# A softmax on negated scores with the attention sink as a 129th column of each head's tile

## The chip, the cores and the metric

The kernel runs on one core of a Trainium2 chip. The metric is the device time of one execution in microseconds (us). The kernel before takes 1183.58 us, the median of three runs (1183.52 to 1184.87).

A core has five engines with a queue of instructions each, which start in order and wait for each other through semaphores: TensorE (PE in the profile; the loading of its weights has a row of its own, PEld), VectorE (DVE), ScalarE (ACT), GpSimd (POOL) and SyncE (SP, which here issues DMAs).

## What is computed

One decoder layer on 1024 positions of width 1024 in float32: two token mixers on one input projection, and behind them a convolutional gated MLP. The change lies in the first mixer, sliding-window attention with 8 query heads, 2 key heads, head width 64 and a window of 128 positions in blocks of 128. Each head has a learned sink: one more score, which takes part in the softmax and has no value row.

```python
scores = jnp.einsum('bnqhgd,bnkhd->bnhgqk', qb, kb) * (HEAD_DIM ** -0.5)
alibi = -slopes[:, :, None, None] * dist[None, None]
scores = jnp.where(valid, scores + alibi, NEG_INF)
probs = jax.nn.softmax(jnp.concatenate([scores, sink], axis=-1), axis=-1)[..., :-1]
out = jnp.einsum('bnhgqk,bnkhd->bnqhgd', probs, vb)
```

## The kernel before, in words

The program runs in stages: the key, value and query projections (to some 50 us), the attention (some 50 to 180 us, with the projection of u and then of the second mixer's v woven in), and the second mixer, gates, merge and MLP to the end. Matrix products are made from a high and a low part of each operand (three products in place of one), so each product is preceded by a split: ScalarE writes the high part (copy_hi, L89), VectorE or GpSimd subtracts it from the value for the low part.

The attention is a loop over sixteen softmax blocks: two halves of four heads, and in each half eight blocks of 128 queries. Since a query sees 128 keys, of the block before and its own, the scores of both key blocks are merged into one tile of 128 columns per head. The tile c holds 128 queries (partitions) by four heads by 128 columns, with three buffers.

The loop (L647 to 685) is written out by hand as a software pipeline, and each engine runs its part in that order. Pass n holds, in this order:

- s_mm(n): scores on TensorE into PSUM (tile sc, two matmul lines, L439 and L442).
- s_mask(n): VectorE merges the two halves (L457) and adds the distance penalty ali, which gives c (L458). In blocks 0 and 8, which have no block before them, it is one addition (L453) and a selection on GpSimd (L454).
- s_exp(n-1): four exponentials on ScalarE, one for each head, with the negated maximum as bias and an accumulated sum (L476); the exponential of the sink's part (L478); on VectorE the sum of both (L479) and the reciprocal (L480); on GpSimd the multiplication of c by it (L481).
- s_max(n): VectorE's maximum over 128 columns (L465), the minimum of its negative and of the negated sink (L466), and sink minus maximum (L467). These last two and L479 work on 128 partitions by 4 numbers, with both inputs in SBUF.
- pv_mm(n-4): probabilities times values on TensorE (L517).
- filler: pieces of other projections on TensorE, by the table FILL.
- p_trans(n-2): four transposes of c on TensorE (L487), in which c is the operand that is loaded as weights and ident the moving one.
- pv_out(n-4): ScalarE copies half of the product (tile o, L527), VectorE adds the other half into ya (L530).
- the norm of new q: a square on ScalarE (L276), a sum and a scaling on VectorE (L281, L282), a power on GpSimd (L283).
- p_split(n-2): the split of the transposed probabilities (ch on ScalarE by L89, cl on VectorE, L496), and on GpSimd four selections that part them into the two key blocks (eh, ch, el, cl; L503 and L505).
- weights(n): the split of loaded weights, with the subtraction on GpSimd (L110, L193). A buffer that it frees is loaded again by SyncE (L99).
- the projection u times rstd_b on VectorE (uT, L679) in passes where it is complete; q's transposes and split for block n+2 (L295, L89, L304), and the q norm's product (qr, L289).

So on VectorE, L479 and L480 of block n-1 stand between L458 and L465 of block n. On ScalarE, the exponentials of block n-1 stand behind the split of q for block n+1. On GpSimd, L481 stands ahead of the power, the selections and the subtractions of its pass. PSUM tiles of TensorE's next product come free when VectorE or ScalarE has read them.

Of the kernel before, what the change touches and what calls it, by code (L numbers as in the profile page):

```python
# [10 lines left out]
F = mybir.dt.float32  # L11
R = mybir.dt.float32r
U8 = mybir.dt.uint8
AF = mybir.ActivationFunctionType
ALU = mybir.AluOpType
AX = mybir.AxisListType
# [7 lines left out]
NEG = -1e30  # L24
# [10 lines left out]
def build(tc, a):  # L35
    nc = tc.nc
    ctx = ExitStack()
    with ctx, tc.manual_schedule(engines={mybir.EngineType.PE}):
        body(ctx, tc, nc, a)


def body(ctx, tc, nc, a):
    L, H = slice(0, 512), slice(512, 1024)
    base = ctx.enter_context(tc.tile_pool(name="base", bufs=1))
# [6 lines left out]
    def nm(s):  # L51
        uid[0] += 1
        return f"{s}_{uid[0]}"
# [26 lines left out]
    def PH(s):  # L80
        if psum.get("H") is None:
            return PS(s)[:, 0:512]
        return psum["H"].tile([128, 512], F, tag="H", name=nm(s))
# [30 lines left out]
    cp = base.tile([128, 194], F, name="cp")  # L114
    sink_b = base.tile([128, 8], F, name="sink_b")
# [19 lines left out]
    def rms_rows(pb, col, hs=(0, 1)):  # L135
# [6 lines left out]
        for h, p in zip(hs, pb):  # L142
# [12 lines left out]
    kgq = at.tile([128, 1], F, name="kgq")  # L155
    eps_x = at.tile([128, 8], F, name="eps_x")
    nsink = at.tile([128, 8], F, name="nsink")
# [8 lines left out]
    ali = kp.tile([128, 8, 128], F, name="ali")  # L166
    nc.gpsimd.affine_select(out=ali[:, 0:4, :], in_=rstd_b[:, 0:128].unsqueeze(1).to_broadcast([128, 4, 128]),
                            pattern=[[0, 4], [1, 128]], compare_op=ALU.is_gt, fill=0.0, base=0,
                            channel_multiplier=-1)
# [57 lines left out]
    for k in range(8):  # L227
# [3 lines left out]
        for c in xcuts[k] if k in xcuts else (slice(0, 512), slice(512, 1024)):  # L231
# [3 lines left out]
                                           op0=ALU.mult, op1=ALU.subtract)  # L235
        for s in range(8):
            o = pkv[s // 4][:, (s % 4) * 256:(s % 4 + 1) * 256]
            c = slice(s * 128, (s + 1) * 128)
# [22 lines left out]
    st = {}  # L261
# [62 lines left out]
    q_proj(1)  # L324
    ss8 = pa.tile([128, 8], F, name="ss8")
    nc.vector.tensor_scalar(nsink, sink_b, -1.0, None, op0=ALU.mult)
    nc.vector.tensor_scalar(kgq, cp[:, 184:185], cp[:, 185:186], 0.125, op0=ALU.mult, op1=ALU.mult)
    nc.vector.tensor_copy(ss8, p_ssq[:, 0:16].rearrange("p (s two) -> p s two", two=2)[:, :, 0])
    rsqrt_cols(rstd, ss8, 8, D)
    nc.vector.tensor_scalar(eps_x, ss8, EPS / D, EPS * EPS, op0=ALU.mult, op1=ALU.add)  # L330
# [1 line left out]
    for h in range(2):  # L332
# [3 lines left out]
                                axis=AX.X, op=ALU.add)  # L336
# [87 lines left out]
    tm = tm_cm.__enter__()  # L424
# [21 lines left out]
    def s_mask(n):  # L446

        half, b = divmod(n, 8)
        p4 = st.pop(("ps", n))
        hs = slice(4 * half, 4 * half + 4)  # L450
        c = tm.tile([128, 4, 128], F, tag="c", name=nm("c"), bufs=3)
        if b == 0:
            nc.vector.tensor_tensor(c, p4[:, :, 0:128], ali[:, hs, :], op=ALU.add)  # L453
            nc.gpsimd.affine_select(out=c, in_=c, pattern=[[0, 4], [-1, 128]], compare_op=ALU.is_ge,  # L454
                                    fill=NEG, base=0, channel_multiplier=1)
        else:
            nc.vector.copy_predicated(p4[:, :, 128:256], msk, p4[:, :, 0:128])  # L457
            nc.vector.tensor_tensor(c, p4[:, :, 128:256], ali[:, hs, :], op=ALU.add)  # L458
        st[("c0", n)] = c

    def s_max(n):
        hs = slice(4 * (n // 8), 4 * (n // 8) + 4)
        c = st.pop(("c0", n))
        sm = tm.tile([128, 4, 4], F, tag="sm", name=nm("sm"), bufs=3)
        nc.vector.tensor_reduce(sm[:, 0, :], c, axis=AX.X, op=ALU.max)  # L465
        nc.vector.scalar_tensor_tensor(sm[:, 0, :], sm[:, 0, :], -1.0, nsink[:, hs], op0=ALU.mult, op1=ALU.min)  # L466
        nc.vector.tensor_tensor(sm[:, 2, :], sink_b[:, hs], sm[:, 0, :], op=ALU.add)  # L467
        st[("c", n)] = (c, sm)

    last_exp, last_sel = [None], [None]  # L470

    def s_exp(n):
        c, sm = st[("c", n)]
        m, den, es = sm[:, 0, :], sm[:, 1, :], sm[:, 2, :]
        for i in range(4):
            last_exp[0] = nc.scalar.activation(c[:, i, :], c[:, i, :], AF.Exp, bias=m[:, i:i + 1],  # L476
                                               accum_out=den[:, i:i + 1])
        nc.scalar.activation(es, es, AF.Exp)  # L478
        nc.vector.tensor_tensor(den, den, es, op=ALU.add)  # L479
        nc.vector.reciprocal(den, den)  # L480
        nc.gpsimd.tensor_tensor(c, c, den.unsqueeze(2).to_broadcast([128, 4, 128]), op=ALU.mult)  # L481

    def p_trans(n):
        c = st.pop(("c", n))[0]
        p = PH("pt")
        for i in range(4):
            nc.tensor.transpose(p[:, i * 128:(i + 1) * 128], c[:, i, :], ident)  # L487
        st[("pt", n)] = p.rearrange("p (h q) -> p h q", q=128)
# [158 lines left out]
    for n in range(20):  # L647
        if n < 16:
            s_mm(n)
            s_mask(n)  # L650
        if 0 <= n - 1 < 16:
            s_exp(n - 1)
        if n < 16:
            s_max(n)
# [3 lines left out]
        if 0 <= n - 2 < 16:  # L658
            p_trans(n - 2)
# [1318 lines left out]
def layout(x, mix_norm, w_in, q_norm, k_norm, sinks, sgu_norm, w_s, b_s,  # L1978
           w_oa, w_ob, w_out, ffn_norm, w_up, conv_w, conv_b, w_down):
    c = np.ascontiguousarray  # L1980
    x, w_in, w_oa, w_ob, w_out = (np.asarray(t)[0] for t in (x, w_in, w_oa, w_ob, w_out))
    w_up, w_down, conv_w, conv_b = (np.asarray(t)[0] for t in (w_up, w_down, conv_w, conv_b))
    mix_norm, ffn_norm, q_norm, k_norm = (np.asarray(t)[0] for t in (mix_norm, ffn_norm, q_norm, k_norm))
    sinks, sgu_norm, w_s, b_s = (np.asarray(t)[0] for t in (sinks, sgu_norm, w_s, b_s))

    def tiles(w, nk):
        n = w.shape[1] // 128
        return c(w.reshape(nk, 128, n, 128).transpose(2, 1, 0, 3))

    def pairs(w):  # L1990
        t = w.reshape(2, 2, 128, 4, 2, 128).transpose(4, 0, 2, 3, 1, 5).reshape(2, 2, 128, 1024)
        return np.stack([t[0, 1], t[0, 0], t[1, 0], t[1, 1]])

    def rows(w):
        return c(w.reshape(2, 4, 128, 2, 256).transpose(3, 2, 0, 1, 4).reshape(2, 128, 2, 8, 128))

    qcols = np.concatenate([np.arange(h * 64, h * 64 + 64) for h in HP])
    xT = x.T.reshape(8, 128, S)
    wk = w_in[:, 512:768].reshape(8, 128, 256)
    up_order = np.stack([np.arange(NPAIR), np.arange(NPAIR) + NPAIR], 1).reshape(-1)  # L2000
    wup = tiles(w_up, 8)[up_order]

    def pcol(v):
        return v.reshape(-1, 128).T

    cwp = conv_w.reshape(3, 44, 128)[:, up_order].transpose(2, 1, 0).reshape(128, 132)
    cbp = pcol(conv_b)[:, up_order]
    bsr = np.repeat(b_s.reshape(4, 2, 128).transpose(1, 0, 2).reshape(2, 512), 64, axis=0)
    qk = np.stack([np.tile(q_norm, 2), np.tile(k_norm, 2)], axis=1)
    q = np.arange(128)[:, None]  # L2010
    j = np.arange(128)[None, :]
    dist = np.where(j <= q, q - j, q - j + 128).astype(np.float32)
    slopes = np.array([2.0 ** -(h + 1) for h in SP], np.float32)
    ali = -slopes[None, :, None] * dist[:, None, :]
    return {
        "xw": c(np.concatenate([mix_norm.reshape(8, 128, 1), wk, xT], axis=2)),
        "wq": rows(w_in[:, qcols]),
        "wvs": rows(w_in[:, 1280:1792]),
        "wu": tiles(w_in[:, 768:1280], 8),
        "wga": tiles(w_in[:, 1792:2816], 8),  # L2020
        "wgb": tiles(w_in[:, 2816:3840], 8),
        "wb": c(np.stack([pairs(w_ob), pairs(w_oa[qcols])])),
        "wout": tiles(w_out, 8),
        "wup": wup,
        "wdown": c(w_down.reshape(NPAIR, 128, 1024)),
        "ws": c(w_s.transpose(2, 0, 1)),
        "cp": c(np.concatenate([pcol(ffn_norm), cwp, cbp, qk, pcol(mix_norm)], axis=1)),
        "sink": c(np.broadcast_to(sinks[SP], (128, 8))),
        "rb": c(np.concatenate([np.broadcast_to(sgu_norm, (128, 512)), bsr], axis=1)),
        "ident": np.eye(128, dtype=np.float32),  # L2030
        "ali": c(ali),
    }
# [13 lines left out]
```

## Time and profile before

| | |
|---|---|
| median of 3 runs | 1183.58 us (1183.52 to 1184.87) |
| span of the profiled execution | 1183.5 us |
| TensorE busy | 1170.3 us (99%) |
| weight load | 990.4 us (84%) |
| VectorE | 874.5 us (74%) |
| ScalarE | 566.5 us (48%) |
| GpSimd | 631.8 us (53%) |

The profiled execution's own time is its span, 1183.5 us; the median of the runs lies 0.1 us beside it. Times in rows of a timeline are us from the span's start; a row has start, length, engine, line, operation, output and inputs by tile name, shapes, and in brackets how long the engine stood idle before and what ended that. A group row has a count, then busy time and mean ns. PE's busy time is that of overlapping matmuls, so a busy PE is not PE at its peak.

### The profile page before, as it was taken

The page shows a single profiled execution, that of the slowest core. Times are in us where ns is not written, and L with a number is a line of the kernel's source. Part 1 is how long each engine was busy: PE and PEld are TensorE (multiplying, and loading weights), DVE is VectorE, ACT ScalarE, POOL GpSimd, SP SyncE. Part 2 cuts the span into 40 slices and gives each one's busy share as a digit, 9 for nine tenths or more (in the row PEclk, how much of TensorE's full clock was granted, in tenths as well). Part 3 has the DMA queues.
Part 4 walks back from the last instruction along what each step waited for, and adds up shares of the span by engine and source line. Part 5 has one row for each costly group of instructions (what it writes and reads, how often), then busy time and mean ns, then how long its engine had stood idle before and what let it go on. Part 6 is the DMA issues. An engine that isn't in the chain of part 4 may idle for free.

```text
span 1183.5 us, 15928 instructions
## 1 busy us (share of the span) xinstructions
PE 1170.3 (99%) x5842; PEld 990.4 (84%) x5842; DVE 874.5 (74%) x1037; ACT 566.5 (48%) x878; POOL 631.8 (53%) x435
## 2 busy tenths in 40 slices
PE   8999999999999999999999999999999999999998
PEld 8989989988888878888878888888888888888887
DVE  7798975743536776678788788877888797875674
ACT  8555667644336653335444443444444445425331
POOL 2467685488884764444867677776767541000000
PEclk9999999999999999999999999999999999999999
DMA  7110136157556654454545445455555268975471
GB/s 272 37 55 19 54 130 228 56 168 239 161 160 204 233 193 154 146 176 132 138 129 169 118 149 152 142 141 134 166 137 160 72 219 287 365 232 196 155 231 67
DMA packets 80942, 188.66 MB, mean 159 GB/s; under 512 B 9184, under 2 KB 16864, under 8 KB 80736
## 3 DMA queue, kind: packets, MB, share of 16 engines
q1 hardware_dynamic: 73008, 167.58, 40.7%
q0 software_dynamic: 7456, 15.73, 8.0%
q10 hardware_dynamic: 400, 4.33, 1.1%
q8 instruction: 46, 0.75, 0.3%
q14 instruction: 32, 0.26, 0.1%
HBM read 146.97 MB, written 49.02 MB: 166 GB/s over the span
## 4 chain that ended last, share of the span: by engine, by line
PE 82%; DVE 4%; POOL 3%; ACT 2%; issue 2%; DMA 1%; DVEq 0%; POOLq 0%; SPq 0%; ACTq 0%
PE pz L1060 50%; PE pd L1855 10%; PE pdy L1855 8%; PE px L95 2%; PE px L93 2%; PE px L94 2%; PE pu L95 1%; PE pu L93 1%; PE pu L94 1%; PE pv L517 1%; PE pq L93 1%; PE pq L95 1%; PE pq L94 1%; DVE xa L621 1%; DMA lq<-wup 0%
## 5 line engine op out<-in xcount | busy, mean ns | idle before, releaser
L1060 PE MATMUL pz<-T,qh 128*128 128x512 f32 x472 | 145.6, 390 | 0.0
L1060 PE MATMUL pz<-B,ph 128*128 128x512 f32 x352 | 109.7, 393 | 0.7 <-ACT x L1695 0.7
L1060 PEld LDWEIGHTS pz<-T,qh 128*128 128x128 f32 x472 | 88.4, 188 | 18.6 <-ACT u L885 0.3
L1019 POOL TENSOR_TENSOR pl<-lp,ph 128x1024 fp32r<-128x1024 f32 x30 | 73.2, 2439 | 52.9 <-ACT ph L89 52.9
L1060 PE MATMUL pz<-T,ql 128*128 128x512 f32 x236 | 91.8, 389 | 0.0
L1019 POOL TENSOR_TENSOR ql<-lq,qh 128x1024 fp32r<-128x1024 f32 x30 | 76.8, 2559 | 9.1 <-ACT qh L89 9.1
L1060 PEld LDWEIGHTS pz<-B,ph 128*128 128x128 f32 x352 | 65.1, 188 | 16.7 <-ACT x L1695 3.8
L1078 DVE TENSOR_TENSOR pz<-pz,rstd_b 128x1024 f32<-128x1024 f32 x60 | 73.9, 1232 | 4.6 <-ACT rstd_b L143 2.5
L1060 PE MATMUL pz<-T,s3h 128*128 128x512 f32 x232 | 71.4, 389 | 0.0
L1060 PE MATMUL pz<-y,wjh 128*128 128x512 f32 x224 | 69.5, 391 | 0.6 <-POOL y L1233 0.3
L1060 PE MATMUL pz<-B,pl 128*128 128x512 f32 x176 | 68.6, 390 | 0.0
L1855 PE MATMUL pd<-bh,ah 128*128 128x512 f32 x176 | 68.5, 389 | 0.0
L1855 PE MATMUL pd<-bl,ah 128*128 128x512 f32 x176 | 68.5, 389 | 0.0
L1855 PE MATMUL pd<-bh,al 128*128 128x512 f32 x176 | 68.5, 389 | 0.0
L1060 PE MATMUL pz<-T,AX 128*128 128x512 f32 x264 | 63.4, 389 | 0.0
L1060 PE MATMUL pz<-B,AX 128*128 128x512 f32 x264 | 63.4, 389 | 0.0
L1019 POOL TENSOR_TENSOR s3l<-lq,s3h 128x512 fp32r<-128x512 f32 x20 | 26.0, 1298 | 62.3 <-ACT s3h L89 62.3
L1060 PEld LDWEIGHTS pz<-T,AX 128*128 128x128 f32 x264 | 49.5, 188 | 10.3
L1060 PEld LDWEIGHTS pz<-B,AX 128*128 128x128 f32 x264 | 49.6, 188 | 10.3
L89 ACT ACTIVATE AX<-lr 128x1024 fp32r<-128x1024 f32 x22 | 23.4, 1063 | 70.9 <-POOL lr L621 70.9
L621 DVE TENSOR_TENSOR pz<-pz,u 128x512 f32<-128x512 f32 x37 | 25.9, 700 | 42.5 <-ACT u L1072 36.2
L1550 DVE SCALAR_TENSOR_TENSOR tg<-pz,cp,tg 128x1023 f32<-128x1023 f32 (+1 forms) x44 | 56.2, 1278 | 0.8
(359 smaller groups left out, 3597.6 us busy)
## 6 DMA issues: line engine op xcount, KB each, us to landing
lp<-wup SPq DMA_DIRECT2D x22, 512.0 KB, 3.8
lq<-wup SPq DMA_DIRECT2D x22, 512.0 KB, 4.2
ra<-wdown SPq DMA_DIRECT2D x44, 256.0 KB, 4.9
b<-T SPq DMA_DIRECT2D x44, 256.0 KB, 3.5
lq<-wup POOLq DMA_DIRECT2D x42, 256.0 KB, 5.3
B<-tv SPq DMA_DIRECT2D x33, 256.0 KB, 2.0
T<-tt SPq DMA_DIRECT2D x33, 256.0 KB, 2.1
b<-B SPq DMA_DIRECT2D x33, 256.0 KB, 3.0
```

Source lines behind the costliest of these rows:

```text
L89: return nc.scalar.activation(dst, src, AF.Copy, scale=scale)
L93: nc.tensor.matmul(out, wh, mh, start=first, stop=False, **kw)
L94: nc.tensor.matmul(out, wh, ml, start=False, stop=False, **kw)
L95: nc.tensor.matmul(out, wl, mh, start=False, stop=last, **kw)
L517: nc.tensor.matmul(o, vhl[:, kb, g, :], w[:, 2 * g:2 * g + 2, :], start=i == 0 and g == 0, stop=i == len(ops) - 1, skip_group_check=True)
L621: eng.tensor_tensor(out, x, y, op=op)
L1019: nc.gpsimd.tensor_tensor(l, r, h.bitcast(F), op=ALU.subtract)
L1060: nc.tensor.matmul(o, p[:, k, :], m, start=not more and k == 0 and j == 0, stop=k == nk - 1 and j == 2, skip_group_check=True)
L1078: nc.vector.tensor_tensor(z, z, rstd_b, op=ALU.mult)
L1550: nc.vector.scalar_tensor_tensor(t[:, j:], p[:, 0:1024 - j], cw[:, ci, 2 - j:3 - j], t[:, j:], op0=ALU.mult, op1=ALU.add)
L1855: nc.tensor.matmul(o[d], p[:, k - k0, m], q[:, k - k0, :], start=new and k == 0 and j == 0, stop=k == HK - 1 and j == 2, skip_group_check= ...
```

## The change

The scores are negated from the start: the factor 0.125 in kgq, which scales the keys, becomes -0.125, the host's table ali changes sign, and the masked value in blocks 0 and 8 becomes positive. The tile c gets a 129th column for each head (its rows now start every 516 bytes instead of 512; the tile has 2064 bytes on each partition instead of 2048), into which ScalarE copies the negated sink at the start of s_mask. One minimum over 129 columns replaces the maximum and the two operations behind it. The exponentials run over 129 columns with scale -1, so that their accumulated sum holds the sink's part; the sink's own exponential and the addition go. The operations on the 128 score columns (L454, L458, L481, the transposes) now work on rows with a gap of one column.

```diff
-    nc.vector.tensor_scalar(kgq, cp[:, 184:185], cp[:, 185:186], 0.125, op0=ALU.mult, op1=ALU.mult)
+    nc.vector.tensor_scalar(kgq, cp[:, 184:185], cp[:, 185:186], -0.125, op0=ALU.mult, op1=ALU.mult)
...
-        c = tm.tile([128, 4, 128], F, tag="c", name=nm("c"), bufs=3)
+        cs = tm.tile([128, 4, 129], F, tag="c", name=nm("c"), bufs=3)
+        c = cs[:, :, 0:128]
+        nc.scalar.copy(cs[:, :, 128], nsink[:, hs])
...
-                                    fill=NEG, base=0, channel_multiplier=1)
+                                    fill=-NEG, base=0, channel_multiplier=1)
...
     def s_max(n):
-        hs = slice(4 * (n // 8), 4 * (n // 8) + 4)
-        c = st.pop(("c0", n))
-        sm = tm.tile([128, 4, 4], F, tag="sm", name=nm("sm"), bufs=3)
-        nc.vector.tensor_reduce(sm[:, 0, :], c, axis=AX.X, op=ALU.max)
-        nc.vector.scalar_tensor_tensor(sm[:, 0, :], sm[:, 0, :], -1.0, nsink[:, hs], op0=ALU.mult, op1=ALU.min)
-        nc.vector.tensor_tensor(sm[:, 2, :], sink_b[:, hs], sm[:, 0, :], op=ALU.add)
-        st[("c", n)] = (c, sm)
+        cs = st.pop(("c0", n))
+        sm = tm.tile([128, 2, 4], F, tag="sm", name=nm("sm"), bufs=3)
+        nc.vector.tensor_reduce(sm[:, 0, :], cs, axis=AX.X, op=ALU.min)
+        st[("c", n)] = (cs, sm)
...
         for i in range(4):
-            last_exp[0] = nc.scalar.activation(c[:, i, :], c[:, i, :], AF.Exp, bias=m[:, i:i + 1],
+            last_exp[0] = nc.scalar.activation(cs[:, i, :], cs[:, i, :], AF.Exp, bias=m[:, i:i + 1], scale=-1.0,
                                                accum_out=den[:, i:i + 1])
-        nc.scalar.activation(es, es, AF.Exp)
-        nc.vector.tensor_tensor(den, den, es, op=ALU.add)
         nc.vector.reciprocal(den, den)
         nc.gpsimd.tensor_tensor(c, c, den.unsqueeze(2).to_broadcast([128, 4, 128]), op=ALU.mult)
...
-    ali = -slopes[None, :, None] * dist[:, None, :]
+    ali = slopes[None, :, None] * dist[:, None, :]
```

On VectorE, pass 6 of the loop stood like this before, from the scores' merge to the split of block 4's probabilities (sm_1127 is block 5's tile of small numbers, sm_1227 block 6's):

```order
L457 COPY_PREDICATED sc_1207<-msk,sc_1207 128x4x128
L458 TENSOR_TENSOR c_1216<-sc_1207,ali 128x512
L479 TENSOR_TENSOR sm_1127<-sm_1127 128x4
L480 RECIPROCAL sm_1127<-sm_1127 128x4
L465 TENSOR_REDUCE sm_1227<-c_1216 128x4
L466 SCALAR_TENSOR_TENSOR sm_1227<-sm_1227,nsink 128x4
L467 TENSOR_TENSOR sm_1227<-sink_b,sm_1227 128x4
L530 TENSOR_TENSOR ya_682<-pv_1231,o_1282 64x2x128 x2
L281 TENSOR_REDUCE qss_1289<-qsq_1287 128x4
L282 TENSOR_SCALAR qss_1289<-qss_1289,eps_x 128x4
L496 TENSOR_TENSOR cl_1294<-pt_1265,ch_1293 128x512
```

The same place now, with the line numbers of the changed kernel (L459, L460, L477, L466, L527 and L493 are the former L457, L458, L480, L465, L530 and L496; sm_1113 and sm_1210 are blocks 5 and 6):

```order
L459 COPY_PREDICATED sc_1191<-msk,sc_1191 128x4x128
L460 TENSOR_TENSOR c_1200<-sc_1191,ali 128x4x128
L477 RECIPROCAL sm_1113<-sm_1113 128x4
L466 TENSOR_REDUCE sm_1210<-c_1200 128x4
L527 TENSOR_TENSOR ya_682<-pv_1212,o_1263 64x2x128 x2
L281 TENSOR_REDUCE qss_1270<-qsq_1268 128x4
L282 TENSOR_SCALAR qss_1270<-qss_1270,eps_x 128x4
L493 TENSOR_TENSOR cl_1275<-pt_1246,ch_1274 128x512
```

The three operations on 128 by 4 numbers that have two inputs in SBUF are gone, and the reciprocal stands directly behind the addition of ali; the rest keeps its order.

On ScalarE, pass 7 stood like this before, from the split of block 4's transposed probabilities on (ch_1293; qs_1306 is the split of a later block's q):

```order
L89 ACTIVATE ch_1293<-pt_1265 128x512
L89 ACTIVATE qs_1306<-pqt_1303 64x256 x2
L476 ACTIVATE c_1216,sm_1227<-c_1216,sm_1227 128x128 x4
L478 ACTIVATE sm_1227<-sm_1227 128x4
L527 COPY o_1388<-pv_1337 64x256 x2
```

And now (c_1303 is block 7's tile, c_1200 block 6's):

```order
L89 ACTIVATE ch_1274<-pt_1246 128x512
L89 ACTIVATE qs_1287<-pqt_1284 64x256 x2
L453 COPY c_1303<-nsink 128x4
L475 ACTIVATE c_1200,sm_1210<-c_1200,sm_1210 128x129 x4
L524 COPY o_1366<-pv_1315 64x256 x2
```

The sink's exponential behind the four of block 6 is gone; in its stead the copy for block 7 stands ahead of them. It waits for the multiplication on GpSimd that used the same of the three buffers last, block 4's. The orders on TensorE, GpSimd and SyncE are as they were.

More of the change, by code (lines that the diff above doesn't have):

```diff
@@ L458, in s_mask @@
             nc.vector.tensor_tensor(c, p4[:, :, 128:256], ali[:, hs, :], op=ALU.add)
-        st[("c0", n)] = c
+        st[("c0", n)] = cs
     def s_max(n):
-        hs = slice(4 * (n // 8), 4 * (n // 8) + 4)
-        c = st.pop(("c0", n))
-        sm = tm.tile([128, 4, 4], F, tag="sm", name=nm("sm"), bufs=3)
-        nc.vector.tensor_reduce(sm[:, 0, :], c, axis=AX.X, op=ALU.max)
-        nc.vector.scalar_tensor_tensor(sm[:, 0, :], sm[:, 0, :], -1.0, nsink[:, hs], op0=ALU.mult, op1=ALU.min)
-        nc.vector.tensor_tensor(sm[:, 2, :], sink_b[:, hs], sm[:, 0, :], op=ALU.add)
-        st[("c", n)] = (c, sm)
+        cs = st.pop(("c0", n))
+        sm = tm.tile([128, 2, 4], F, tag="sm", name=nm("sm"), bufs=3)
+        nc.vector.tensor_reduce(sm[:, 0, :], cs, axis=AX.X, op=ALU.min)
+        st[("c", n)] = (cs, sm)
     last_exp, last_sel = [None], [None]
     def s_exp(n):
-        c, sm = st[("c", n)]
-        m, den, es = sm[:, 0, :], sm[:, 1, :], sm[:, 2, :]
+        cs, sm = st[("c", n)]
+        m, den, c = sm[:, 0, :], sm[:, 1, :], cs[:, :, 0:128]
         for i in range(4):
-            last_exp[0] = nc.scalar.activation(c[:, i, :], c[:, i, :], AF.Exp, bias=m[:, i:i + 1],
+            last_exp[0] = nc.scalar.activation(cs[:, i, :], cs[:, i, :], AF.Exp, bias=m[:, i:i + 1], scale=-1.0,
                                                accum_out=den[:, i:i + 1])
-        nc.scalar.activation(es, es, AF.Exp)
-        nc.vector.tensor_tensor(den, den, es, op=ALU.add)
         nc.vector.reciprocal(den, den)
@@ L483, in p_trans @@
     def p_trans(n):
-        c = st.pop(("c", n))[0]
+        c = st.pop(("c", n))[0][:, :, 0:128]
         p = PH("pt")
```

## The prediction

> **What bounds the kernel now.** I read the busy time by stretch first. The change touches only the sixteen softmax blocks, so 50 to 170 us matters.
>
> ```profile
> 50.00:170.00 120.00, 117.52 (x815) 106.95 (x815) 107.26 (x229) 73.32 (x244) 80.92 (x89) 1.00 0.16 58
> ```
>
> The columns behind the length are PE, PEld, DVE, ACT and POOL busy, the granted clock, DMA share, GB/s. TensorE is at 98% at full clock; VectorE has 89%. TensorE sets the end, and freeing VectorE is worth what TensorE waits for it. So next I read the TensorE timeline at its idle places (the bracket is the idle time and who ended it).
>
> ```profile
> 60.49 0.36 PE L439 MATMUL sc<-kT,qs 128*128 128x256 f32 x1 [0.60 <-DVE c L458]
> 83.05 0.35 PE L439 MATMUL sc<-kT,qs 128*128 128x256 f32 x1 [0.41 <-DVE uT L679]
> 97.68 0.35 PE L517 MATMUL pv<-eh,vhl 128*128 128x256 f32 x1 [0.17 <-DVE ya L530]
> 99.02 0.38 PE L93 MATMUL pq<-wq,x 128*128 128x256 f32 x1 [0.17 <-DVE cl L496]
> 112.84 0.38 PE L93 MATMUL pq<-wq,x 128*128 128x256 f32 x1 [0.18 <-DVE cl L496]
> 141.50 0.36 PE L517 MATMUL pv<-eh,vhl 128*128 128x256 f32 x1 [0.42 <-DVE ya L530]
> 167.27 0.39 PE L517 MATMUL pv<-cl,vhl 128*128 128x256 f32 x1 [0.41 <-POOL cl L505]
> 179.02 0.39 PE L517 MATMUL pv<-cl,vhl 128*128 128x256 f32 x1 [0.54 <-POOL cl L505]
> ```
>
> Idle understates the loss, because matmuls overlap: in the stream a 128x256 matmul shows 0.28 and the next starts 0.11 later, so a stall costs its idle time plus 0.17.
>
> ```profile
> 85.23 0.28 PE L95 MATMUL pq<-wq,x 128*128 128x256 f32 x1
> 85.34 0.28 PE L93 MATMUL pq<-wq,x 128*128 128x256 f32 x1
> ```
>
> Two smaller stalls show in the waits, on the weight load's side (us in total, times, longest):
>
> ```profile
> PEld pt L487 <- POOL c L481: 0.5, 1, 0.5
> PEld pv L517 <- POOL el L503: 0.3, 1, 0.3
> ```
>
> **What the change removes.** The view of tile sm gives each small operation (minimum/median/maximum ns):
>
> ```profile
> L465 DVE TENSOR_REDUCE sm<-c x16: 653/655/687, 55.6 to 158.8; 128x4 f32<-128x512 f32 x16
> L466 DVE SCALAR_TENSOR_TENSOR sm<-sm,nsink x16: 158/600/2199, 56.4 to 159.5; 128x4 f32<-128x4 f32 x16
> L467 DVE TENSOR_TENSOR sm<-sink_b,sm x16: 161/164/968, 56.6 to 161.8; 128x4 f32<-128x4 f32 x16
> L478 ACT ACTIVATE sm<-sm x16: 188/189/193, 58.3 to 163.3; 128x4 f32<-128x4 f32 x16
> L479 DVE TENSOR_TENSOR sm<-sm x16: 152/395/1912, 60.3 to 164.1; 128x4 f32<-128x4 f32 x16
> L480 DVE RECIPROCAL sm<-sm x16: 178/178/180, 60.9 to 164.3; 128x4 f32<-128x4 f32 x16
> ```
>
> L466, L467 and L479 go. They move four numbers and need 0.15 us unhindered, yet last up to 2.2. The timelines of VectorE and GpSimd side by side say why:
>
> ```profile
> 93.23 1.91 DVE L479 TENSOR_TENSOR sm<-sm 128x4 f32<-128x4 f32 x1
> 95.96 0.60 DVE L466 SCALAR_TENSOR_TENSOR sm<-sm,nsink 128x4 f32<-128x4 f32 x1
> 96.60 0.16 DVE L467 TENSOR_TENSOR sm<-sink_b,sm 128x4 f32<-128x4 f32 x1
> 96.68 0.85 DVE L530 TENSOR_TENSOR ya<-pv,o 64x256 f32<-64x256 f32 x2
> 109.38 0.69 DVE L465 TENSOR_REDUCE sm<-c 128x4 f32<-128x512 f32 x1 [0.40 <-POOL c L454]
> 110.10 0.27 DVE L466 SCALAR_TENSOR_TENSOR sm<-sm,nsink 128x4 f32<-128x4 f32 x1
> ```
>
> ```profile
> 92.71 2.42 POOL L110 TENSOR_TENSOR wul<-u,wuh 128x1024 fp32r<-128x1024 f32 x1
> 95.50 1.04 POOL L481 TENSOR_TENSOR c<-c,sm 128x512 f32<-128x512 f32 x1 [0.38 <-DVE sm L480]
> 109.31 1.04 POOL L481 TENSOR_TENSOR c<-c,sm 128x512 f32<-128x512 f32 x1
> ```
>
> L479 ends at 93.23 + 1.91 = 95.14, just behind GpSimd's subtract (92.71 + 2.42 = 95.13); L466 ends at 96.56, just behind the multiply (96.54). A VectorE operation with two SBUF inputs is held until the GpSimd operation is over. The one-input reduction at 109.38 is not: it starts 0.07 behind a multiply and takes 0.69 against 0.655. All three operations that go are of the held kind. So one block frees 0.72 us from L466 and L467 (95.96 to 96.68) and from 0.19 to 1.95 from L479. The held operations being gone, VectorE waits for GpSimd only through data.
>
> The Trainium skill ("SBUF — State Buffer", section "Who interferes with whom") states this as a lock: two SBUF inputs contend with a GpSimd operation that reads SBUF, one input outside the two-port modes doesn't. By that rule the reciprocal, which now stands where L479 stood, isn't held; the trace, where L480 always follows a held operation, can't show it. A rival below prices the opposite.
>
> **First term: the five stalls on VectorE from 83 to 142.** Each ends a run of VectorE work that holds at least one L466 and L467 pair: 0.72 us, or 0.39 in block 8 (110.10 to 110.49, by its 0.27). The losses are 0.58, 0.34, 0.34, 0.35 and 0.59, each below its pair (98 and 99 share one run, which also holds the 1.91). They go: 2.2 us. Next late there is TensorE itself. The one at 60.49 (0.77) I leave: ahead of it VectorE waits for q's norm, two powers in a row on GpSimd of 1 us each, which don't move.
>
> ```profile
> L283 POOL TENSOR_TENSOR qss<-qss,mh 128x4 f32<-128x4 f32 x14 | 14.1, 1010 | 18.7 <-DVE qss L282 17.1 <-DVE sm L466 1.6
> ```
>
> **Second term: the end of the stage, 149 to 179,** where GpSimd comes last:
>
> ```profile
> 149.40 0.64 POOL L505 TENSOR_SCALAR_AFFINE_SELECT ch<-ch 128x512 fp32r<-128x512 f32 x1 [1.64 <-DVE cl L496]
> 154.10 1.04 POOL L481 TENSOR_TENSOR c<-c,sm 128x512 f32<-128x512 f32 x1 [0.37 <-DVE sm L480]
> 157.38 0.64 POOL L505 TENSOR_SCALAR_AFFINE_SELECT ch<-ch 128x512 fp32r<-128x512 f32 x1 [1.64 <-DVE cl L496]
> 159.27 2.44 POOL L193 TENSOR_TENSOR wv<-v,wv 128x1024 fp32r<-128x1024 f32 x1
> 164.35 0.64 POOL L505 TENSOR_SCALAR_AFFINE_SELECT ch<-ch 128x512 fp32r<-128x512 f32 x1 [1.05 <-DVE sm L479]
> 178.00 0.97 POOL L505 TENSOR_SCALAR_AFFINE_SELECT cl<-cl 128x512 fp32r<-128x512 f32 x1
> ```
>
> ```profile
> 159.53 2.20 DVE L466 SCALAR_TENSOR_TENSOR sm<-sm,nsink 128x4 f32<-128x4 f32 x1
> ```
>
> The four idle times, 4.7 us, are all waits for a VectorE that is late through the removed operations (the 2.20 behind the subtract at 159.27 is the largest). From 164.35 GpSimd runs nearly without a break until 178.97, so whatever is gained before moves the last selection (178.00), which TensorE awaits at 179.02. One thing limits this: the weights s are loaded into the buffer that the subtract at 159.27 frees, so they move only with it.
>
> ```profile
> 161.74 0.33 SPq L99 DMA_DIRECT2D s<-ws  x1
> ```
>
> Ahead of that subtract lie the first three of the idle times, 3.65 us; I put GpSimd's advance at 3.7 to 4.7. TensorE needs its last operand earlier too: 2.2 for the first term, 0.3 at pt, 0.58 at 167.27 and 0.2 at el, so 3.3 earlier than now, and the last stall of 0.71 asks for 4.0. GpSimd's 3.7 to 4.7 spans that. I take all four: 0.3 + 0.58 + 0.2 + 0.71 = 1.8 us (0.3 and 0.2 are estimates, rather below the idle rows 0.5 and 0.3).
>
> **Parts at nothing.** ScalarE gives up L478 (0.19) and gets a copy of the same 128x4 size per block; nearest row 0.19, so bounds of -0.1 to +0.2 per block, hidden since ScalarE is busy for 73 of 120. The copy waits for the multiply that last used its c buffer, three blocks back; behind it on ScalarE stand the exponentials, the o copies and the next split, and VectorE's reduction and TensorE would wait for those. But earlier in its queue ScalarE has already waited for the transposes that follow that multiply. The reduction now reads that copy, which stands a whole block's exponentials ahead of the reciprocal that VectorE awaits anyway. Exponentials and reduction grow by 1 in 128: below 1% of their time, on engines with slack. Signs, fill and host tables cost no instruction. The rows of c now start at steps of 516 bytes: no row shows such operands, so zero is taken from the same operations (1.04 for the multiply); its bad end is the last rival.
>
> **Sum.** The profiled execution spans 1183.5, the median is 1183.58, so 0.1 lies around it. 1183.5 - 2.2 - 1.8 + 0.1 = 1179.6. Behind 185 TensorE waits little, and for engines that it feeds itself:
>
> ```profile
> PE pm L93 <- ACT pm L926: 0.5, 1, 0.5
> PE pz L1060 <- ACT x L1695: 0.7, 1, 0.7
> ```
>
> So the gain should reach the end.
>
> **Rivals.** *Only the first term (0.15):* GpSimd advances less than TensorE and stays last, because the s load or ScalarE's copies of the weights hold it. Against it: four idle times of GpSimd sit in the rows. 1183.6 - 2.2 = 1181.4.
>
> *The reciprocal is held (0.08):* it takes over L479's waits, and the multiply's 0.38 of idle stays. The pairs still cover the first term; I halve the second: 1183.6 - 3.1 = 1180.5. The row at 109.38 speaks against it.
>
> *Nothing reaches the end (0.13):* TensorE is 98% busy and its waits turn up elsewhere, on the copy's queue or in a later stage. Between 1181.4 and 1184, middle 1183. Speaking for it: by the medians VectorE gives up 16 x (600 + 164 + 395) ns = 18.5 us, of which I count on only 4.0, so most of it is idle time already.
>
> *Slower (0.06):* the transposes load their weights from c, now in rows off any power of two.
>
> ```profile
> L487 PEld LDWEIGHTS pt<-ident,c x64: 138/140/144, 64.2 to 170.5; 128*128 128x128 f32 x64
> ```
>
> 64 loads on the bounding engine: from 4.0 / 64 = 63 ns more each the gain is eaten, 100 ns or more makes it slower by over 0.2%. Were each doubled, 9.0 us: 1188.6. No row speaks for it.
>
> **Numbers.** The forecast keeps 0.58. About 0.2% (2.4 us) is what a measurement of this kernel tells from no change: faster lies below 1181.2. Faster: 0.58, the held reciprocal's 0.08 and a third of the first-term case: 0.71. Same: two thirds of that, and 0.12 of the nothing case: 0.22. Slower: 0.07. The range runs from 1178.2 (60.49's 0.77 gained too, and the two weight-load stalls costing idle plus 0.17, 1.14 instead of 0.5) to 1182.5, which leaves out slower and most of the nothing case.
>
> **What would show it.** Right: L466, L467 and L479 gone with VectorE's busy time in 50 to 170 some 20 us lower; the reciprocal still near 0.18 us under GpSimd's long subtracts; no idle TensorE at 83, 98, 99, 113 and 141; the wait at 60 still there; the last selection 4 us earlier. Wrong: the reciprocal stretched to 1 us or more; new TensorE waits for ScalarE behind the copy; loads of c above 140 ns; or TensorE early at 180 and no earlier at the end.

## The result, and the profile after

The kernel after takes 1179.13 us, median of 5 runs (1178.76 to 1180.37), beside 1183.73 us for the kernel before (1183.52 to 1184.87, five runs, of which the 1183.58 at the start is the median of three): a ratio of 0.9959, with a 95% interval of 0.9948 to 0.9969. It is faster by 4.6 us, and 1179.6 was forecast. Seven more runs of after on another chip (the eighth experiment) gave 1180.51 beside 1184.16, a ratio of 0.9976 (0.9963 to 0.9989). The twelve runs of after together have the median 1179.6; two of them, 1183.73 and 1183.85, are as long as runs of before, so one execution proves little here, and traces are compared by single waits.

First the stretch of the softmax blocks, in the same columns as before (PE, PEld, DVE, ACT and POOL busy):

```profile
50.00:170.00 120.00, 119.42 (x845) 110.12 (x844) 87.68 (x184) 75.81 (x247) 85.33 (x94) 1.00 0.18 62
```

VectorE falls from 107.26 to 87.68, by 19.6 us; TensorE rises to 99.5% of the stretch. ScalarE shows 2.5 us more, which is later work that now falls into the stretch: over the whole span it is busy for 566.4 us, 566.5 before. In the view of tile sm, what is left for VectorE is one reduction and the reciprocal per block:

```profile
L466 DVE TENSOR_REDUCE sm<-c x16: 658/691/691, 55.5 to 154.6; 128x4 f32<-128x516 f32 x16
L477 DVE RECIPROCAL sm<-sm x16: 166/168/178, 60.1 to 158.5; 128x4 f32<-128x4 f32 x16
```

No reciprocal is held (maximum 178 ns). The timelines of GpSimd and VectorE at the place where L479 took 1.91 us:

```profile
91.88 2.40 POOL L110 TENSOR_TENSOR wul<-u,wuh 128x1024 fp32r<-128x1024 f32 x1
94.23 1.04 POOL L478 TENSOR_TENSOR c<-c,sm 128x512 f32<-128x512 f32 x1
```

```profile
92.43 0.17 DVE L477 RECIPROCAL sm<-sm 128x4 f32<-128x4 f32 x1
92.55 0.69 DVE L466 TENSOR_REDUCE sm<-c 128x4 f32<-128x516 f32 x1
93.15 0.85 DVE L527 TENSOR_TENSOR ya<-pv,o 64x256 f32<-64x256 f32 x2
94.03 0.42 DVE L281 TENSOR_REDUCE qss<-qsq 128x4 f32<-128x256 f32 x1
94.48 0.82 DVE L282 TENSOR_SCALAR qss<-qss,eps_x 128x4 f32<-128x4 f32 x1
```

Under the whole subtract, to 94.28, VectorE runs the reciprocal, a reduction and L527's pair through. The last row is new: L282, which took 0.23 us, is held to 95.30, the end of the multiply (95.27). In the view of its tile:

```profile
L282 DVE TENSOR_SCALAR qss<-qss,eps_x x16: 220/230/821, 39.0 to 138.7; 128x4 f32<-128x4 f32 x16
```

Of TensorE's waits for another engine's work in the stretch, one is left, the one at 60 us (the view of its waits from 50 to 185 us has this single row; the timeline shows the same):

```profile
PE sc L439 <- DVE sm L477: 0.6, 1, 0.6
```

```profile
60.31 0.47 PE L439 MATMUL sc<-kT,qs 128*128 128x256 f32 x2 [0.58 <-DVE sm L477]
```

At the end of the stage, GpSimd's timeline and the load of s:

```profile
154.68 2.42 POOL L193 TENSOR_TENSOR wv<-v,wv 128x1024 fp32r<-128x1024 f32 x1
157.06 1.04 POOL L478 TENSOR_TENSOR c<-c,sm 128x512 f32<-128x512 f32 x1
160.80 1.09 POOL L789 TENSOR_SCALAR_AFFINE_SELECT s<-s 128x1024 f32<-128x1024 f32 x1 [0.82 <-DMA s<-ws]
172.78 1.16 POOL L502 TENSOR_SCALAR_AFFINE_SELECT cl<-cl 128x512 fp32r<-128x512 f32 x1
```

```profile
157.13 0.33 SPq L99 DMA_DIRECT2D s<-ws  x1
```

The subtract stands 4.59 us earlier (159.27 before), the load of s behind it 4.61 earlier, and the last selection 5.22 earlier (178.00). GpSimd now waits 0.82 for that load, as the prediction's limit said, but TensorE's last operand no longer comes late.

Where VectorE's other time went, two rows of the waits say (before, the same two were 9.9 and 3.1 us):

```profile
POOL c L478 <- DVE sm L477: 14.5, 7, 4.4
DVE qs L304 <- ACT qs L89: 14.1, 9, 2.5
```

VectorE now waits for ScalarE's split of q, and GpSimd for sums of exponentials: both ran ahead into idle time, with TensorE as the bound.

The matmuls are the same 5842 in the same order in every kernel here. So the start-to-start distance of one pair can be followed through the kernels, in ns, worked out from the trace's start times (places named by before's time; "restart" is the distance behind the stalled matmul; the kernels are before, after, and the experiments in their order below):

```
place            before before2  held  free  min  sum  wide  late after2 scalar  after
 83.05              683     679   489    29  564  194   696    29     29    346     28
 97.68              446     391   117   116  117  116   296   116    116    117    116
 99.02              446     447   444   117  442  118   440   118    117    381    118
 its restart        221     222   223   117  223  117   223   118    118    221    117
112.84              452     405   213   118  113  114   415   113    113    117    113
 its restart        223     221   222   116  141  120   223   121    120    117    120
141.50              693     711   391   115  446  190   639   116    117    264    117
pt 162.76           510     488   239   230  230  230   410   230    229    231    230
167.27              688     664   505   118  118  116   633   116    118    118    116
 its restart        222     222   224   118  118  117   228   117    116    118    117
el 177.98           364     327   225   118  118  115   176   115    116    118    116
 its restart        223     224   226   117  117  118   222   118    117    117    118
179.02              815     811   813   119  783  120   812   119    120    119    120
 its restart        229     222   223   117  222  113   224   114    114    117    113
sum               6215    6034  4554  1665 3752 1898  5637  1660   1660   2501   1659
593               1070    1632   227  1377  227  283   617   348    697   1114    226
```

The sum falls from 6215 to 1659 ns: 4.56 us, about as much as the medians differ by (4.6). The first five stalls give 2.43 with their restarts, the last four 2.12. The two profiled executions themselves differ by 6.1 us: 4.8 lie in the attention (from the 301st matmul to the 1238th), and 1.25 at 593 and 612 us, which vary between executions of one kernel, as the experiments below show.

### The profile page after: what moved, and what is told of

It reads as the page before. It is cut to its first block, busy times and chain, and to the rows that moved or that the text cites. A ratio compares the mean times of both kernels' runs of the same rounds, so it can differ in the third digit from the quotient of the medians.

```text
span 1177.4 us, 15845 instructions
## 1 busy us (share of the span) xinstructions
PE 1166.7 (99%) x5842; PEld 989.2 (84%) x5842; DVE 852.7 (72%) x989; ACT 566.4 (48%) x878; POOL 631.5 (54%) x435
## 4 chain that ended last, share of the span: by engine, by line
PE 90%; DVE 2%; POOL 1%; ACT 1%; issue 1%; DVEq 0%; POOLq 0%; ACTq 0%
PE pz L1057 54%; PE pd L1852 10%; PE pdy L1852 8%; PE px L95 2%; PE px L93 2%; PE px L94 2%; PE pv L514 1%; PE pu L93 1%; PE pu L95 1%; PE pu L94 1%; PE pq L95 1%; PE pq L94 1%; PE pq L93 1%; PE pt L484 1%; PE sc L439 1%
## 5 line engine op out<-in xcount | busy, mean ns | idle before, releaser
L1547 DVE SCALAR_TENSOR_TENSOR tv<-pz,cp,tv 128x1023 f32<-128x1023 f32 (+1 forms) x44 | 56.3, 1279 | 0.8
```

The costliest lines, as they stand in the source:

```text
L1547: nc.vector.scalar_tensor_tensor(t[:, j:], p[:, 0:1024 - j], cw[:, ci, 2 - j:3 - j], t[:, j:], op0=ALU.mult, op1=ALU.add)
```

## The experiments

Theory: VectorE operations with two SBUF inputs are held until GpSimd's operation ends, and the gain is that none is left between a block's reduction and what TensorE awaits. Rivals: the number of operations counts, not their kind; the gain comes from the chain, since the sink's exponential and its sum no longer stand ahead of the reciprocal; the wider rows of c cost something that hides part of the gain.

**Before, once more.**

> The kernel before once more, for a second profile of it. Between the two profiles of before and after TensorE also lost its waits for the tile x at 593 us (0.84 and 0.11) and at 612 us (0.30), far behind the change. Theory: these belong to single executions of the kernel before, of the 1184.9 us kind, and an execution near 1183.6 us doesn't have them; the waits in the attention (83 to 179 us) stand as in the first profile. Rival: they belong to the kernel before and the change removed them too: they are there again, in an execution of 1183.6 us.

1184.16 us (10 runs), ratio 1.0001 (0.9992 to 1.001). All nine places are back within 60 ns. A wait at the start of the MLP is not: here 1.24 us, in the first profile of before 0.68.

```profile
592.92 0.73 PE L1060 MATMUL pz<-B,ph 128*128 128x512 f32 x2 [1.24 <-ACT x L1695]
```

**Held operations put back, idle.** After, with three operations of the removed kind at the removed places.

```diff
         nc.vector.tensor_reduce(sm[:, 0, :], cs, axis=AX.X, op=ALU.min)
...
+        nc.vector.tensor_tensor(dm[:, 0, :], sm[:, 0, :], nsink[:, hs], op=ALU.min)
+        nc.vector.tensor_tensor(dm[:, 1, :], sink_b[:, hs], dm[:, 0, :], op=ALU.add)
...
+        nc.vector.tensor_tensor(dm[:, 0, :], dm[:, 0, :], dm[:, 1, :], op=ALU.add)
         nc.vector.reciprocal(den, den)
```

> The changed kernel with three idle operations per block on VectorE, put where the removed ones stood: 128 by 4 numbers, two SBUF inputs each, results used by nothing. Theory (the removed operations cost time because an operation with two SBUF inputs is held while GpSimd works): the waits of TensorE come back, 1183.0 to 1183.7 us, and the idle operations last 0.6 us and more behind the reduction, up to 2 us under GpSimd's long subtracts. Rival 1 (what costs is the number of small operations, 0.15 us each): the same time as the sibling with one-input operations, both about halfway back, 1180.5 to 1182. Rival 2 (the gain comes from the chain: the sink's exponential and its sum leave the way to the reciprocal): 1179.1, as the changed kernel, since nothing waits for the idle operations.

1184.1 us (11 runs), ratio 0.9996 (0.9988 to 1.0005): the gain is gone, and with it the rival of the chain, by which this run takes 1179.1. The view of the idle tile, min/median/max in ns:

```profile
L469 DVE TENSOR_TENSOR dm<-sm,nsink x16: 158/531/2295, 55.4 to 157.4; 128x4 f32<-128x4 f32 x16
L470 DVE TENSOR_TENSOR dm<-sink_b,dm x16: 161/163/964, 55.6 to 159.7; 128x4 f32<-128x4 f32 x16
L482 DVE TENSOR_TENSOR dm<-dm x16: 152/380/1865, 59.3 to 162.1; 128x4 f32<-128x4 f32 x16
```

Nothing but the trio itself reads these results, and the three are held like L466, L467 and L479. In this execution 2.9 us of the stalls return (4554 against 1659), with the last one in full:

```profile
176.96 0.50 PE L520 MATMUL pv<-cl,vhl 128*128 128x256 f32 x2 [0.53 <-POOL cl L508]
```

**The same places, one input.** Three idle reciprocals in their stead (the cut is against the run before).

```diff
-        nc.vector.tensor_tensor(dm[:, 0, :], sm[:, 0, :], nsink[:, hs], op=ALU.min)
-        nc.vector.tensor_tensor(dm[:, 1, :], sink_b[:, hs], dm[:, 0, :], op=ALU.add)
+        nc.vector.reciprocal(dm[:, 0, :], sm[:, 0, :])
+        nc.vector.reciprocal(dm[:, 1, :], sink_b[:, hs])
...
-        nc.vector.tensor_tensor(dm[:, 0, :], dm[:, 0, :], dm[:, 1, :], op=ALU.add)
+        nc.vector.reciprocal(dm[:, 0, :], dm[:, 1, :])
```

> The changed kernel with three idle reciprocals per block at the same three places, 128 by 4 numbers, one SBUF input each. Theory: not held, about 0.12 to 0.17 us each, 0.4 us per block against the 1.2 us and more that VectorE got free: 1179.0 to 1179.8. Rival 1 (number of operations): the same as the sibling with two inputs, 1180.5 to 1182. Rival 2 (chain): 1179.1, as the changed kernel.

1180.97 us (11 runs), ratio 0.9971 (0.9962 to 0.998): 1.2 us above the expected range.

```profile
L469 DVE RECIPROCAL dm<-sm x16: 170/178/179, 55.7 to 155.3; 128x4 f32<-128x4 f32 x16
L470 DVE RECIPROCAL dm<-sink_b x16: 145/146/148, 55.8 to 155.4; 128x4 f32<-128x4 f32 x16
L482 DVE RECIPROCAL dm<-dm x16: 166/168/170, 59.6 to 157.7; 128x4 f32<-128x4 f32 x16
```

None of 48 is stretched, and the stalls stay away (1665 ns). The same count of operations at the same places is 3.1 us apart by kind: the rival "number of operations", which asks for the same time in both runs, falls. The time itself lies in the range that this rival gave (1180.5 to 1182); why it isn't nearer to after's is taken up at the end of the next section.

**Only the minimum takes the sink in.** L466 goes; sink minus minimum, the sink's exponential and the addition stay (sm with two buffers, for room).

```diff
+        nc.vector.tensor_tensor(sm[:, 2, :], sink_b[:, hs], sm[:, 0, :], op=ALU.add)
...
-            last_exp[0] = nc.scalar.activation(cs[:, i, :], cs[:, i, :], AF.Exp, bias=m[:, i:i + 1], scale=-1.0,
+            last_exp[0] = nc.scalar.activation(c[:, i, :], c[:, i, :], AF.Exp, bias=m[:, i:i + 1], scale=-1.0,
...
+        nc.scalar.activation(es, es, AF.Exp)
+        nc.vector.tensor_tensor(den, den, es, op=ALU.add)
```

> Only the minimum includes the 129th column: L466 goes, but the sink's difference (L467), its exponential and the addition (L479) stay as in the kernel before, and the exponentials run over 128 columns. Theory: L467 now stands first behind the reduction and is held there by GpSimd's multiplication in L466's stead (0.6 us), and L479 is held as before, so a block gets only some 0.1 us free: 1182.8 to 1183.6. Rival 1 (number of operations): one of three gone, 1182.2 or so. A gain of 2 us or more would speak against the hold.

1181.76 us (9 runs), ratio 0.998 (0.997 to 0.9989): 2.6 us less than before's 1184.37 on the same chip, more gain than expected. By the expectation's own words a gain of 2 us or more speaks against the hold, so the hold itself has to be looked at. The groups of before's L466, from the view by lines (busy time in us, mean ns), and of the operation that is now first behind the reduction:

```profile
L466 DVE SCALAR_TENSOR_TENSOR sm<-sm,nsink 128x4 f32<-128x4 f32 x16 | 10.5, 655 | 0.5
```

```profile
L468 DVE TENSOR_TENSOR sm<-sink_b,sm 128x4 f32<-128x4 f32 x16 | 10.5, 655 | 0.5
```

The hold is there, and passes on whole to whichever held operation comes first: 655 ns on average in both. VectorE is freed of little (107.3 us in the stretch, 104.3 here), yet five of the nine stalls go. So what failed is not the hold but the count of the gain by the time that is held: a stall is a few tenths of lateness, and a little taken off each block can be enough for it. Why it is these five was not tried.

**Only the sum takes the sink in.** The maximum, its sign and L466 stay; L467, the sink's exponential and L479 go. The cut shows s_max against after; the scores keep their sign, as in before.

```diff
-        nc.vector.tensor_reduce(sm[:, 0, :], cs, axis=AX.X, op=ALU.min)
+        nc.vector.tensor_reduce(sm[:, 0, :], cs[:, :, 0:128], axis=AX.X, op=ALU.max)
+        nc.vector.scalar_tensor_tensor(sm[:, 0, :], sm[:, 0, :], -1.0, nsink[:, hs], op0=ALU.mult, op1=ALU.min)
```

> Only the accumulated sum includes the 129th column (scores keep their sign, the copy takes the sink itself): L467, the sink's exponential and L479 go, the maximum over 128 columns and L466 stay. Theory: the waits at 98, 99 and 113 go, since L479's 1.91 and 0.61 stand ahead of them; those at 83 and 141 shrink by 0.27 each and keep 0.3; block 15's L466 stays held for some 2 us, so the end of the stage gains 0.5 to 1.2: together 2.0 to 2.7 less than before, 1181.0 to 1181.7. Rival 1 (number of operations): two of three gone, 1180.6. Rival 2 (chain): the whole gain, 1179.1.

1179.49 us (6 runs), ratio 0.9966 (0.9953 to 0.9978): the whole gain as far as the interval tells, more than expected, and by the time alone what the rival of the chain gave for this run; the first held trio is what speaks against that rival. Only 0.17 us stays at 83 and 0.07 at 141. L466 (here L468) is still held, for 1.87 us behind GpSimd's subtract in the last block:

```profile
155.33 1.87 DVE L468 SCALAR_TENSOR_TENSOR sm<-sm,nsink 128x4 f32<-128x4 f32 x1
```

```profile
154.75 2.43 POOL L193 TENSOR_TENSOR wv<-v,wv 128x1024 fp32r<-128x1024 f32 x1
```

It ends at 157.20, the subtract at 157.18, and TensorE doesn't notice. By the sums of the table the two halves take 2.5 and 4.3 us off, both together 4.6. They aren't terms of a sum: five of the nine stalls (98, 113, 163, 167 and 178) go with either half alone.

**Only the wider rows.** Before, with c in rows of 129 columns (and two buffers of sm in place of three, for room).

```diff
-        c = tm.tile([128, 4, 128], F, tag="c", name=nm("c"), bufs=3)
+        c = tm.tile([128, 4, 129], F, tag="c", name=nm("c"), bufs=3)[:, :, 0:128]
...
-        sm = tm.tile([128, 4, 4], F, tag="sm", name=nm("sm"), bufs=3)
+        sm = tm.tile([128, 4, 4], F, tag="sm", name=nm("sm"), bufs=2)
```

> The kernel before with c's rows at steps of 129 columns and nothing else (the 129th column isn't used; the small tile sm has two buffers in place of three, for space). Theory: rows off a power of two cost nothing, 1183.3 to 1184.0, the transposes' loads of c at 140 ns, the multiplication at 1.04 us. Rival: they cost, and the change won more than it shows: 1185 or more, by 63 ns per load some 4 us.

1184.8 us (11 runs), ratio 1.0006 (0.9997 to 1.0015): no price that can be told from none, though the interval reaches to 1.8 us. The operations on c themselves, in the view of that tile:

```profile
L487 PEld LDWEIGHTS pt<-ident,c x64: 137/140/145, 63.7 to 170.3; 128*128 128x128 f32 x64
L481 POOL TENSOR_TENSOR c<-c,sm x16: 1037/1040/1042, 60.8 to 166.9; 128x512 f32<-128x512 f32 x16
L458 DVE TENSOR_TENSOR c<-sc,ali x14: 691/692/693, 59.2 to 157.6; 128x512 f32<-128x512 f32 x14
```

The loads stay at 140 ns, the multiplication at 1.04 us and the addition at 0.69.

**The wait at 60 us.** After, with the norm's product of the first new q behind the mask of block 1 rather than ahead of it.

```diff
             s_mask(n)
+        if n == 1:
+            q_norm(4)
...
-        for q in [3] + q_new if n == 0 else q_new:
+        for q in [3] if n == 0 else q_new:
```

> The changed kernel with one operation moved: the product of q's norm for block 4 (L289), which in pass 0 stands on VectorE ahead of block 1's merge and waits there for two powers on GpSimd, now stands behind it. The prediction left TensorE's wait at 60 us (0.77, 0.74 measured after the change) to those two powers. Theory: the wait goes, 0.74 less: 1178.4. Rival: it stays, or TensorE finds the next wait at once: 1179.1.

1180.01 us (5 runs, 1178.09 to 1181.56), ratio 0.9964 (0.9952 to 0.9977). The wait goes: the 150 matmuls around it take 19.52 us instead of 20.11, and the shift is kept to the end of the attention (start-to-start from the 301st matmul to the 1238th: 131.35 in after, 130.76 here). That shows that it was q's norm, as the prediction had it. The median can't be told from after's; five runs don't resolve 0.6 us.

**After, once more.**

> The kernel after once more, unchanged, beside the next run. Theory: what the change itself moves is the stretch from 83 to 181 us, and its eight stalls are gone again (each gap between matmuls there back at 0.12 us). The waits near 593 and 612 us, absent in the first profile of after and 1.2 to 1.7 us in those of before, belong to the execution: they may come back here, up to 1.5 us, with a span up to 1179. Rival: the change removes these two as well; then they are absent again and the span is 1177.4 within 0.6. Median of the runs 1179.1 to 1180.0 by either, unless the first median was a lucky draw.

1180.51 us (7 runs, 1179.06 to 1183.85), ratio 0.9976 (0.9963 to 0.9989), 0.5 above the expected range: a gain of 3.65 us here, 4.6 in the first measurement. The nine stalls are gone again (1660 ns). At 593 TensorE loses 0.47 us that it didn't lose in the first profile of after, and 0.17 more at 612. So these waits belong to the execution: the kernel before shows 1070 and 1632 ns at that place in two profiles, after 226 and 697.

**One tensor and two constants.** After, with three idle scalings.

```diff
...
+        nc.vector.tensor_scalar(dm[:, 0, :], sm[:, 0, :], 0.5, 0.25, op0=ALU.mult, op1=ALU.add)
+        nc.vector.tensor_scalar(dm[:, 1, :], sink_b[:, hs], 0.5, 0.25, op0=ALU.mult, op1=ALU.add)
...
+        nc.vector.tensor_scalar(dm[:, 0, :], dm[:, 1, :], 0.5, 0.25, op0=ALU.mult, op1=ALU.add)
```

> After, with three idle operations per block on 128x4 numbers at the removed places, each with one tensor input and two constants (result times 0.5 plus 0.25, read by nobody). In after the scaling L282, one tensor input and a pointer to a column, was stretched three times, to 0.50, 0.54 and 0.82 us, each time to the end of a GpSimd multiply. Theory A, this kind of operation is held whatever its scalar: the first of the three is stretched to 1 us and more in some blocks, some of the eight stalls return, 1182 to 1184.3 us. Theory B, it is the pointer that is read beside the tensor: all 48 stay below 0.25 us, the stalls stay away, and the time is that of the run with three idle reciprocals, 1179 to 1181 us.

1181.73 us (11 runs, 1180.21 to 1182.21), ratio 0.9977 (0.9968 to 0.9986).

```profile
L469 DVE TENSOR_SCALAR dm<-sm x16: 165/536/2221, 55.6 to 156.0; 128x4 f32<-128x4 f32 x16
L470 DVE TENSOR_SCALAR dm<-sink_b x16: 155/156/1085, 55.7 to 158.2; 128x4 f32<-128x4 f32 x16
L482 DVE TENSOR_SCALAR dm<-dm x16: 158/389/1872, 59.5 to 160.7; 128x4 f32<-128x4 f32 x16
```

Held like operations with two tensor inputs, though they read one and no pointer: theory A. The time lies between the two theories (from 1182 and up to 1181), so it is the hold in this view that decides. It is the kind of operation, not the count of tensors read. Its stalls return at 83, 99 and 141 (0.84 us in all), fewer than the first held trio's 2.9. The holds are alike and the stalls aren't: a stall needs a chain that ends late, and which one does can turn on a few tenths. That last is a reading, not shown by a run of its own.

## Why the prediction was right

**The held operations.** Right: the idle trios differ in kind alone, and one kind costs the gain. "VectorE waits for GpSimd only through data" was wrong, though: L282 has one tensor input and is held too, 3 of 16 times in after (0.50, 0.54 and 0.82 us in place of 0.23). In before none of 16 was: there it never started under one of GpSimd's subtracts, multiplies or selections; with the removed operations gone it does. No stall of TensorE came of it. Nor does every operation of GpSimd hold: beside its powers (L131 and L283, 1.0 us and more) L282 keeps its 0.23 us, three times in before and three in after, with 0.08 to 0.51 us of the power still to run.

**The reciprocal.** Right: 48 idle ones and after's 16 stay below 0.18 us. The page "SBUF — State Buffer" of the Trainium skill, section "Who interferes with whom", agrees: one SBUF input outside the two-port modes doesn't contend. The same section names scaling by scalars among the operations that can take both ports if their operands allow it; the traces agree with 1.87 and 2.22 us for four numbers on a partition, and I had read past it for L282.

**First term, 2.2.** Measured 2.43. The five stalls went by 0.66, 0.33, 0.33, 0.34 and 0.58, within 0.08 of the forecast; what it lacked is the restart: behind a stall that ends in a run of 128x256 matmuls the next one comes 0.22 later instead of 0.12. Two of the five have it, 0.2 us. Two more, at 98 and 141, have 0.19 instead of 0.12, another 0.15 us that the table leaves out.

**Second term, 1.8.** Measured 2.12: 0.28, 0.57, 0.25 and 0.70, with 0.32 for three restarts. GpSimd's advance was put at 3.7 to 4.7; the subtract came 4.59 earlier and the last selection 5.22. The size was right, but where it came from was luck. The prediction took it from the idle times from 149 on. In after, GpSimd is 3.2 us ahead before them (the selection at 145.12 stands at 141.92) and gains 0.4 at the next multiply. The three idle times ahead of the subtract, 3.65 us, give only about 1.0, because 2.6 us are idle again, mostly in these two:

```profile
149.62 1.04 POOL L478 TENSOR_TENSOR c<-c,sm 128x512 f32<-128x512 f32 x1 [0.68 <-DVE sm L477]
151.94 0.64 POOL L500 TENSOR_SCALAR_AFFINE_SELECT eh<-ch 128x512 fp32r<-128x512 f32 x1 [1.28 <-ACT ch L89]
```

That TensorE asks for 4.0 and gets it was the closest call: in the run with the minimum alone the last stall still stands (783 ns of 815).

**The sum.** The gain was forecast at 4.0 and is 4.56 in these traces, larger by the 0.5 of restarts; the medians give 4.6 and, in the second measurement, 3.65, so they don't tell the two apart. That "0.1 lies around" the span was wrong: the runs list a span beside each time, 1177.4 beside 1179.13 for the profiled one, so 1.7 us lies around it. Before's second profile has 1183.6 beside 1185.33; so its first span of 1183.5 stands for some 1185.2 us, 1.5 more than the median. Two mistakes cancelled in the start point: a span was taken for a time, 1.7 too little, of an execution that was 1.5 longer than the median. So by luck the sum starts where the median lies. What is left is the 0.5 of restarts by which 1179.6 lies above 1179.13, less than one execution varies by.

**Parts at nothing.** The sink's copy (0.20 us a block, L478 had 0.19) and the 129th column (389 ns for an exponential, 388 before) cost next to nothing, and no wait of TensorE, VectorE or GpSimd for the copy stands in the view of the waits. The misaligned rows cost nothing (the rival that made it slower: loads of 137 to 143 ns against 138 to 144).

**"So the gain should reach the end."** It does, but "behind 185 TensorE waits little" was read from one execution: the wait at 593 varies by half a us between two profiles of one kernel and by 1.4 over all of them, and runs of one kernel by up to 5.

**Of 18.5 us of VectorE, 4.0.** Right in its size. Most of the rest became idle time of VectorE, as the prediction counted on: its busy time in the stretch fell by 19.6 us, and its waits for ScalarE's split of q alone grew by 11. Wrong was how I thought of parts: both half changes were expected to give their share of the stalls, and gave 2.6 and 4.9 us by the medians against a whole of 4.6 (3.65 in the second measurement).

What stays open: five kernels here (wide, both held trios, the free one, the minimum alone) run their matmul stream a little slower where nothing waits. The 206 matmuls between the stalls at 113 and 141 take 27.94 to 27.98 us in them, 27.72 to 27.75 in the other six. In three of them it goes on to 590 us, 0.5 to 0.7 us over that stretch. Of the time that the first held trio loses this is up to 1.2 us, and it would account for most of the 0.7 between the free trio and after in the attention. What sets it was not tried, and no single edit divides the two groups. One thing does: by the sizes of c, sm and dm, the tiles behind them (ch, cl, eh, el and o) lie 32 bytes further on in each partition in these five (ch from byte 181664 in the built programs) than in the other six (181632). Whether that is the cause is open.

## What to carry to other kernels

Look at operations that take many times their least time for a handful of numbers: line up their ends with GpSimd's, and replace them by a form that isn't held (a reduction or a reciprocal here) or fold them into a neighbour, rather than making them smaller. Count the gain at the bounding engine's stalls, one by one with their restarts, not in the busy time freed. And don't add up the parts of such a change: removing one held operation hands the hold to the next, while a small shift may free a whole chain.

## What the runs showed of the hardware

- A VectorE scaling by two constants on 128x4 numbers is held by GpSimd as long as one with two tensors: up to 2.22 us against 0.16. A reciprocal or a reduction isn't: 0.145 to 0.18 us in 64 cases, 0.65 to 0.69.
- A maximum or minimum of 128x512 or 128x516 takes about 655 or about 690 ns, whatever the width. It takes 685 to 692 where only the reciprocal stands between it and the addition that writes c and it starts 0.034 us behind that addition: in after and its repeat, the sum alone and the late norm, 512 numbers in one of them and 516 in the others. In the last block of the same kernels, 0.52 us behind, it takes 656 to 662, and so it does in the others, 651 to 662, except in blocks 0 and 8 (675 to 692 in every kernel). So the prediction's 1% for the 129th column isn't what sets it. What stands just ahead of it on VectorE seems to; no run tried that by itself.
- GpSimd's powers don't hold VectorE's scaling L282: 0.23 us in the six cases, three in before and three in after, that ran beside one.
- Rows at steps of 516 bytes: no difference on TensorE's weight loads, GpSimd or VectorE to 1%.
- After a stall, the second matmul of 128x256 starts late as well: 0.22 to 0.23 us behind the first at five of the nine stalls and 0.19 at two more, 0.12 where nothing stalls.
